# A hybrid encoder block on one core: branch A's query tiles taken two at a time in TensorE's hand-written order

## The chip, the cores and the metric

The kernel runs on one core of one Trainium2 chip. The metric is the time of one execution on the device in microseconds (us), the median of several runs. Lower is better. The engines are called as in the profile: PE (TensorE; PEld is its weight load), DVE (VectorE), ACT (ScalarE), POOL (GpSimd) and SP (SyncE, which issues the DMAs).

## The reference

One encoder layer is applied to a prompt of 2048 tokens and a sample of 512 tokens, with shared weights; 16 learned meta tokens stand ahead of each. Two attention branches are computed side by side, gated, projected and merged:

```python
u = rms_norm(h, norm_g)
proj = u @ w_in
qa, ka, va, za, qb, kb, vb, zb, ga, gb = jnp.split(proj, cuts, axis=-1)
o_a = neighbourhood_attention(qa, ka, va, na_rpb, n)      # 8 heads of 64, on a grid 64 wide
o_b = window_attention(qb, kb, vb, t5_bias, sink, n)      # 8 query heads, 2 key heads, +-128 tokens
y_a = (o_a * jax.nn.silu(za)) @ w_proj_a
y_b = (o_b * jax.nn.silu(zb)) @ w_proj_b
merged = jax.nn.sigmoid(ga) * y_a + jax.nn.sigmoid(gb) * y_b
h = h + merged @ w_out
return rms_norm(h[:, N_META:], final_g)
```

In branch A a grid token attends to a neighbourhood of 8 rows by 16 columns of the grid and to the meta tokens, with a learned bias. In branch B a token attends to 128 tokens on either side, the meta tokens and a sink. All is float32; each matmul operand is split into a high and a low float32r part, and products are summed from three matmuls (high by high, high by low, low by high).

## The kernel before, in words

The 2560 tokens are five windows of 512 (window 0 is the sample). A first phase, some 985 us long, computes the projections and writes queries, keys, values and gates to DRAM. The second phase does the attention, and between its pieces the dense work: the gates of the last window, the output projections of both branches, the last matmul and the final norm. After it comes a short end for the last window.

The attention's work is cut into units, one query tile of 128 each. `units` lists them window by window: first 32 units of branch A (four pairs of heads p, two heads h, four column groups g; `unit_a`, line 1047), then 16 units of branch B (two key heads gh, four tiles n, two head pairs i; `unit_b`, line 1143). A unit is a generator that gives back control after each of five steps:

- load: the DMAs of its keys, values and bias, where it is the first that needs them (g == 0);
- scores: two matmuls into a bank of PSUM (lines 1089, 1090; for branch B lines 1195, 1196, for two heads), the bias and the maximum on DVE (line 1020), the exponential with its sum on ACT (line 1027);
- normalise: the reciprocal on DVE (line 1031) and a multiplication into the tile `pr`, on DVE (line 1038), for g == 1 on ACT (line 1036);
- transposes: two to four blocks of `pr` through PE into a bank of PSUM called `tp` (line 1113; branch B line 1215, 1218), copied by ACT into the high part `ph` (line 1116) and by DVE into the low part `pl` (line 1117; branch B lines 1222, 1223, and 1232 to 1234 for the meta tokens, `pms`);
- products: values by probabilities into the one bank of `ps_o` (lines 1128, 1130; branch B lines 1239 to 1244). In branch A the four units of a head add up in the bank: the unit with g == 0 issues no product, and after g == 3 the bank is emptied by ACT (line 1134) and DVE (line 1136). In branch B each unit empties the bank: ACT copies one half (`ol`, line 1246), and DVE adds the halves with two additions (`y`, line 1249).

The first unit of B of each window gives control back once more, between the scores of its two heads (line 1191).

PSUM holds two banks for scores (`ps_s`), three for `tp` (`ps_p`; in branch A every third unit's scores use one of these), one for products (`ps_o`) and two for dense work (`ps_d`). A dense step is six matmuls of 128x512 (two calls of `mm3`, lines 144 to 146). A bank of a branch's output projection (`psa`, `psb`) takes two steps, one of the last matmul (`pso`) four. A finished `psb` bank is multiplied by the gate's tile `sgb`, which a DMA loads, on DVE (line 1304). The weights come through `Weights`: ACT writes the high part (line 198), POOL the low part (line 199). `phases` says which dense work belongs to which window and branch, `fill(amount)` runs as many dense steps as have come due. With a share of 0.5 for each half of a unit of A, one unit gets one dense step; in window 0, with 40 steps for 32 units, it is 0.625 each; in B one unit gets two steps. Five steps (`HELD`) are left over from B of window 0 for A of window 1, and so on.

The loop at line 1521 writes PE's order out by hand (`manual_schedule` for PE). The other engines' orders, SP's with its DMAs among them, are laid out by the framework from the order of the program and its own estimate of times. For the unit i, the loop asks for: the load of i + 4, the scores of i + 2, the normalising of i + 1, a fill, the transposes of i, a fill, and the products of i - 1. PE's order is so: scores of i + 2, transposes of i, a dense step, products of i - 1. Just before branch B one unit of B gets an extra step, because of its extra stop.

Of the kernel before, what the change touches and what calls it, by code (L numbers as in the profile page):

```python
# [95 lines left out]
def encoder_block(ctx: ExitStack, tc: tile.TileContext, xT, x_end, w_in, w_pa, w_pb, w_o, norm_g, final_g,  # L96
# [42 lines left out]
    def move(out, in_):  # L139
        last_move[0] = nc.sync.dma_start(*(f32(a) if a.dtype == F32R else a for a in (out, in_)))  # L140
        return last_move[0]
# [66 lines left out]
    class Weights:  # L208
# [16 lines left out]
        def next(self):  # L225
            i = self.i
            self.i += 1
            self.fetch(i + 2)
            self.split(i + 1)
            return self.wt.pop(i)  # L230
# [1211 lines left out]
    def phases(w, br):  # L1442

        if br == "a":
            if w == 0:
                yield from islice(gates, GATES_A)
            else:
                yield from dense_pb(w - 1)
                yield from dense_out(w - 1, range(0, 4))
        elif w == 0:  # L1450
            yield from gates
            open_dense()
            yield from dense_pa(0)
        else:
            yield from dense_out(w - 1, range(4, 8))
            pa = dense_pa(w)
            yield from islice(pa, 1)
            yield from with_fill(pa, dense_fin(w - 1))
# [7 lines left out]
    units = []  # L1466
# [31 lines left out]
    with tc.manual_schedule(engines={E.PE}):  # L1498
        N = len(units)
        dense, key, due = iter(()), None, 0.0  # L1500

        def fill(amount):
            nonlocal due
            due += amount
            while due >= 1 and next(dense, "end") != "end":
                due -= 1

        for i in range(1, 4):
            next(units[i][2])
        for _ in islice(gates, GATES_0 - 4):  # L1510
            pass
        for i in range(2):
            next(units[i][2])
        for _ in islice(gates, 4):
            pass
        vbm = vbm_d.rearrange("m g (h f) -> m g h f", h=2)
        for h in range(2):
            for r, part in ((0, 0), (32, 0), (64, 1)):
                move(vms[r + 16 * h : r + 16 * h + 16, :, h], vbm[:, :, part, :])
        next(units[0][2])  # L1520
        for i in range(N):
            br, w, _, weight = units[i]
            if key != (br, w):
                key, dense = (br, w), chain(dense, phases(w, br))
            if i == N - LAST:
                lo_eng[0] = nc.vector
            share = COUNT.get(key, 32) * weight / 32 / 2
            if i + 4 < N:
                next(units[i + 4][2])
            if i + 2 < N:  # L1530
                next(units[i + 2][2])
            if i + 1 < N:
                next(units[i + 1][2])
            fill(share)
            next(units[i][2])
            if [u[0] for u in units[i + 1 : i + 3]] == ["a", "b"]:
                next(units[i + 2][2])
            fill(share)
            if i:
                next(units[i - 1][2])  # L1540
        fill(2)
        next(units[N - 1][2])
        for _ in dense:
            pass
    attn.close()
# [105 lines left out]
```

## Time and profile before

| | us |
|---|---|
| median of 3 runs | 1888.8 (1888.74 to 1891.85) |
| time of the profiled execution | 1891.56 |
| its span from first to last instruction | 1889.7 |
| PE busy in the span | 1860.3 |
| DVE busy | 1316.7 |
| ACT busy | 1144.3 |
| POOL busy | 725.3 |

Branch A's transposes run from 992.8 to 1726.4 us of the span; A's five stretches are about 80 us long each, with B's between.

How to read it: all times are from one profiled execution, in us from the start of its span. A row of the timeline has the start, the duration, the engine, the line of the kernel, the operation, what it writes and what it reads, the shapes, a count (x4: four merged into one row), and in brackets how long the engine stood idle ahead of it and what ended that. The ends of matmuls are modelled, so that durations of neighbours overlap; the distance between two starts is what a matmul took of PE's time. A wait for several things is put down to the one that came last.

### The profile page before, as it was taken

The numbers are of one execution on the slowest core, as the hardware profiler recorded it, in microseconds if no ns is written. First come the engines' busy times: TensorE is split into PE (matmuls) and PEld (weight loads), VectorE is DVE, ScalarE is ACT, GpSimd is POOL, SyncE is SP. The second block draws the span as 40 slices with busy tenths as digits, with TensorE's granted clock in tenths as the row PEclk, the third lists the DMA queues.
The fourth block names the chain that finished last, engine by engine and source line by source line (L and its number), as shares of the span: only waits on it lengthen the run. The fifth ranks groups of instructions, "written<-read, shape, count | busy, mean of one in ns | idle before, by whom it ended". The sixth has DMA issues, their size and how long they took to land. (4 is left out here: it accounts for less than half of the span.)

```text
span 1889.7 us, 29760 instructions
## 1 busy us (share of the span) xinstructions
PE 1860.3 (98%) x9797; PEld 1585.9 (84%) x9797; DVE 1316.7 (70%) x2939; ACT 1144.3 (61%) x2523; POOL 725.3 (38%) x556
## 2 busy tenths in 40 slices
PE   8999999999999999999999999999999999999998
PEld 6898888888888887888878888888888888888886
DVE  8896666556477565444457888878787877888874
ACT  6454444434365443444456797797788778878932
POOL 2005442223202232232324435656744763685420
PEclk9999999999999999999999999999999999999999
DMA  7668666555296777744358878977985997697473
GB/s 262 227 173 306 195 181 191 192 194 179 81 333 228 234 214 203 205 140 156 110 193 311 275 213 263 298 220 247 314 281 177 313 314 226 218 315 257 119 296 138
DMA packets 290385, 424.83 MB, mean 225 GB/s; under 512 B 117416, under 2 KB 162040, under 8 KB 288696
## 3 DMA queue, kind: packets, MB, share of 16 engines
q1 hardware_dynamic: 289944, 422.93, 69.4%
q8 instruction: 78, 1.28, 0.3%
q14 instruction: 75, 0.61, 0.1%
q10 hardware_dynamic: 288, 0.01, 0.0%
HBM read 303.46 MB, written 119.39 MB: 224 GB/s over the span
## 5 line engine op out<-in xcount | busy, mean ns | idle before, releaser
L199 POOL TENSOR_TENSOR wt<-wraw,wt 128x512 fp32r<-128x512 f32 x164 | 213.3, 1319 | 266.5 <-ACT wt L198 264.9
L826 PE MATMUL pa<-u,wt 128*128 128x512 f32 x1008 | 242.7, 390 | 0.0
L826 PE MATMUL pa<-u,x 128*128 128x512 f32 x984 | 237.0, 390 | 1.7 <-ACT u L837 1.7
L198 ACT CAST wt<-wraw 128x512 fp32r<-128x512 f32 x312 | 177.9, 619 | 75.8 <-PE mm L146 37.4
L826 PEld LDWEIGHTS pa<-u,wt 128*128 128x128 f32 x1008 | 188.9, 188 | 39.1
L826 PEld LDWEIGHTS pa<-u,x 128*128 128x128 f32 x984 | 184.4, 188 | 41.1 <-ACT u L837 2.8
L797 POOL TENSOR_TENSOR s<-wraw,raw 128x512 f32<-128x512 f32 x40 | 58.3, 1458 | 274.5 <-DVE x L199 274.5
L144 PE MATMUL mm<-u,wt 128*128 128x512 f32 (+2 forms) x416 | 151.2, 363 | 7.8 <-ACT u L325 7.3
L792 POOL TENSOR_TENSOR s<-raw 128x512 f32<-128x512 f32 x40 | 58.4, 1459 | 255.4 <-DMA raw<-in_w_in_dram 252.1
L146 PE MATMUL mm<-u,wt 128*128 128x512 f32 (+2 forms) x416 | 147.6, 355 | 1.9 <-DVE wt L199 1.9
L145 PE MATMUL mm<-u,wt 128*128 128x512 f32 (+2 forms) x416 | 147.5, 355 | 1.1 <-DVE u L326 1.1
L199 DVE TENSOR_TENSOR wt<-wraw,wt 128x512 fp32r<-128x512 f32 x148 | 107.0, 760 | 49.5 <-ACT wt L198 49.4
L826 PE MATMUL pe<-u,wt 128*128 128x512 f32 x504 | 121.3, 389 | 0.0
L826 PE MATMUL pc<-u,wt 128*128 128x512 f32 x504 | 121.1, 389 | 0.0
L826 PE MATMUL pe<-u,x 128*128 128x512 f32 x480 | 115.3, 389 | 0.0
L826 PEld LDWEIGHTS pc<-u,wt 128*128 128x128 f32 x504 | 94.6, 188 | 19.6
L826 PEld LDWEIGHTS pe<-u,wt 128*128 128x128 f32 x504 | 94.5, 188 | 19.6
L1117 DVE TENSOR_TENSOR pl<-tp,ph 128x384 fp32r<-128x384 f32 (+6 forms) x160 | 94.8, 593 | 20.5 <-ACT ph L1116 18.0
L1116 ACT CAST ph<-tp 128x384 fp32r<-128x384 f32 (+6 forms) x160 | 81.7, 510 | 43.1 <-PE tp L1113 41.6
L144 PE MATMUL pso<-mh,wt 128*128 128x512 f32 x256 | 107.1, 418 | 0.0
L805 POOL TENSOR_TENSOR s<-wraw,s 128x512 f32<-128x512 f32 x40 | 54.9, 1373 | 132.7 <-DVE wt L199 132.7
L826 PEld LDWEIGHTS pe<-u,x 128*128 128x128 f32 x480 | 90.1, 188 | 18.7
(242 smaller groups left out, 4999.6 us busy)
## 6 DMA issues: line engine op xcount, KB each, us to landing
wraw<-in_w_in_dram SPq DMA_DIRECT2D x86, 512.0 KB
qa<-evq SPq DMA_DIRECT2D x20, 1024.0 KB
raw<-in_w_in_dram SPq DMA_DIRECT2D x40, 512.0 KB
q<-qa SPq DMA_DIRECT2D x20, 1024.0 KB
wraw<-in_w_o_dram SPq DMA_DIRECT2D x32, 512.0 KB
kbt<-kb SPq DMA_DIRECT2D x32, 384.0 KB
qb<-evq SPq DMA_DIRECT2D x20, 512.0 KB
ka<-evk SPq DMA_DIRECT2D x20, 512.0 KB
```

The costliest lines, as they stand in the source:

```text
L144: nc.tensor.matmul(ps, wh, uh, start=first, stop=False)
L145: nc.tensor.matmul(ps, wh, ul, start=False, stop=False)
L146: nc.tensor.matmul(ps, wl, uh, start=False, stop=last)
L198: nc.scalar.copy(h, r)
L199: low[0] = (eng or lo_eng[0]).tensor_sub(l, r, f32(h)).ins
L792: eng.tensor_add(s1, a21, a22)
L797: eng.tensor_sub(s3, a11, a21)
L805: eng.tensor_sub(s4, a12, s2)
L826: nc.tensor.matmul(ps, wt[:, a, s], u[:, b, kk, :], start=first and kk == 0 and i == 0, stop=kk == 3 and i == 2, skip_group_check=True)
L1116: nc.scalar.copy(ph_[:kb, a], tb)
L1117: nc.vector.tensor_sub(pl_[:kb, a], tb, f32(ph_[:kb, a]))
```

## The change

The loop takes branch A's units two at a time and leaves branch B's one at a time. For a pair (i, i + 1) of A it asks for: the loads of i + 4 and i + 5, the scores of i + 2, the normalising of i + 1, the products of the last unit of B if one is still open (`behind`), the transposes of i and of i + 1, the scores of i + 3, two dense steps' share, the normalising of i + 2, two more shares (so that a pair gets its two dense steps in one run, in window 0 two or three), and the products of i and i + 1. PE's order is so: scores of i + 2, transposes of i and i + 1, scores of i + 3, two dense steps, products of i and i + 1. At the last pair ahead of B (`change`) the two stops in the first B unit's scores are spread over the pair, and the second unit of B has its scores between the two dense steps. The number of steps of each unit and the dense work are the same.

```diff
         next(units[0][2])
-        for i in range(N):
+        def step(j):
+            if 0 <= j < N:
+                next(units[j][2])
+
+
+        i, behind = 0, -1
+        while i < N:
             br, w, _, weight = units[i]
             if key != (br, w):
                 key, dense = (br, w), chain(dense, phases(w, br))
             if i == N - LAST:
                 lo_eng[0] = nc.vector
             share = COUNT.get(key, 32) * weight / 32 / 2
-            if i + 4 < N:
-                next(units[i + 4][2])
-            if i + 2 < N:
-                next(units[i + 2][2])
-            if i + 1 < N:
-                next(units[i + 1][2])
-            fill(share)
-            next(units[i][2])
-            if [u[0] for u in units[i + 1 : i + 3]] == ["a", "b"]:
-                next(units[i + 2][2])
-            fill(share)
-            if i:
-                next(units[i - 1][2])
+            if br == "a":
+                change = units[i + 2][0] == "b"
+                step(i + 4)
+                step(i + 5)
+                step(i + 2)
+                step(i + 1)
+                step(behind)
+                step(i)
+                step(i + 1)
+                step(i + 2 if change else i + 3)
+                fill(2 * share)
+                if change:
+                    step(i + 3)
+                step(i + 2)
+                fill(2 * share)
+                step(i)
+                step(i + 1)
+                i, behind = i + 2, -1
+            else:
+                step(i + 4)
+                step(i + 2)
+                step(i + 1)
+                fill(share)
+                step(i)
+                fill(share)
+                step(behind)
+                i, behind = i + 1, i
         fill(2)
-        next(units[N - 1][2])
+        step(behind)
         for _ in dense:
             pass
```

## The prediction

> **What bounds the kernel now.** I read the page first: the span, and which engine fills it.
>
> ```profile
> span 1889.7 us, 29760 instructions
> PE 1860.3 (98%) x9797; PEld 1585.9 (84%) x9797; DVE 1316.7 (70%) x2939; ACT 1144.3 (61%) x2523; POOL 725.3 (38%) x556
> ```
>
> TensorE (PE) is the bound. The change touches only the stretches in which branch A runs, one for each of the five windows, so next I asked for the busy times in those five stretches (columns: length, then PE, PEld, DVE, ACT, POOL, the granted clock, DMA share, GB/s). Two of them and the sum of all five:
>
> ```profile
> core 0: us, PE busy (x) PEld busy (x) DVE busy (x) ACT busy (x) POOL busy (x), PEclk, DMA share, GB/s
> 1308.00:1394.00 86.00, 83.69 (x498) 72.11 (x498) 69.77 (x180) 66.13 (x151) 60.88 (x49) 1.00 1.03 316
> 1478.00:1563.00 85.00, 83.15 (x497) 71.68 (x496) 69.69 (x179) 65.56 (x147) 59.10 (x48) 1.00 1.03 315
> sum 414.00, PE 408.47 PEld 355.00 DVE 336.70 ACT 313.27 POOL 267.34; mean PE 81.69 PEld 71.00 DVE 67.34 ACT 62.65 POOL 53.47
> ```
>
> PE is idle for 414.00 - 408.47 = 5.5 us in all of branch A, 4.2 of it in the two quoted stretches (windows 2 and 3), where the DMA share is 1.03. The clock is 1.00, so there is none to win. The instructions of the transposes' line (L1113) say what most of the idle time is: four waits.
>
> ```profile
> L1113 PE MATMUL tp<-ident,pr x528: 270/272/302, 992.8 to 1726.4; 128*128 128x128 f32 x102, 128*96 128x128 f32 x37, 128*104 128x128 f32 x37
> DVE pr L1038: 4.2, 4
> ```
>
> So an order of PE's work can win in two ways: if neighbours in the order cost something where the operation changes, or by taking away those 4.2 us. Everything else it does can only add waits.
>
> **Neighbours.** Per pair of tiles, before: scores, transposes, dense step, products, twice. After: scores, both transposes, scores, two dense steps, both products. The matmuls are the same. The timeline of PE (start, duration; x4 is four merged) shows transposes followed by a dense step, and one place where transposes are followed by scores, as they will be:
>
> ```profile
> 1161.54 0.60 PE L1113 MATMUL tp<-ident,pr 128*96 128x128 f32 x4
> 1161.89 0.48 PE L144 MATMUL psb<-yb,wt 128*128 128x512 f32 x1
> 1162.21 0.40 PE L145 MATMUL psb<-yb,wt 128*128 128x512 f32 x1
> 1162.44 0.40 PE L146 MATMUL psb<-yb,wt 128*128 128x512 f32 x1
> ...
> 1221.58 0.29 PE L1196 MATMUL s<-kbt,q 128*128 128x274 f32 x1
> 1221.71 0.60 PE L1113 MATMUL tp<-ident,pr 128*96 128x128 f32 x4
> 1222.06 0.38 PE L1195 MATMUL s<-kbt,q 128*128 128x274 f32 x1
> 1222.28 0.30 PE L1196 MATMUL s<-kbt,q 128*128 128x274 f32 x1
> ```
>
> Durations have modelled ends; starts are what counts. Four transposes take 0.60 with the last lasting 0.272, so they start (0.60 - 0.272)/3 = 0.109 apart; dense matmuls start 0.23 apart (1162.21 to 1162.44). The first dense matmul looks expensive (0.48), but from the first transpose to the second dense matmul it is 1162.21 - 1161.54 = 0.67, and 4 x 0.109 + 0.23 = 0.67: the switch is free, the long first matmul is only the short last transpose (0.35 - 3 x 0.109 = 0.02) given back. At the second place, 1222.28 - 1221.71 = 0.57 = 4 x 0.109 + 0.13, the 0.13 being what such scores take (1221.58 to 1221.71): free as well. There are 160 tiles, so 80 meetings of transposes and dense work vanish; at the 0.004 us by which these sums are uncertain that is **-0.3 us**, bounds 0 and -1.6 (0.02 each, the one remainder seen).
>
> **From branch B to branch A (4 places).** The diff moves the products of the last tile of B, step(behind), ahead of A's first transposes, before any dense step. Products of B go to the one bank of ps_o, and each tile's products need that bank emptied of the tile before: a copy on ACT (L1246), then two additions on DVE (L1249). Before, one such place on three engines:
>
> ```profile
> 1477.53 0.28 PE L1244 MATMUL ob<-pl,vb 128*64 128x256 f32 x1
> 1477.65 0.40 PE L1089 MATMUL s<-kd,q 128*128 128x512 f32 x1
> 1478.13 0.49 PE L1113 MATMUL tp<-ident,pr 128*128 128x128 f32 x3
> 1479.85 0.28 PE L1239 MATMUL ob<-ph,vb 128*128 128x256 f32 x1
> ...
> 1477.85 0.37 ACT L1246 COPY ol<-ob 64x256 f32<-64x256 f32 x1 [0.30 <-PE ob L1244]
> ...
> 1478.25 0.58 DVE L1249 TENSOR_TENSOR y<-ob,ol 64x128 f32<-64x128 f32 x2 [0.71 <-ACT ol L1246]
> ```
>
> The bank is free at 1478.25 + 0.58 = 1478.83. Today transposes and a dense step lie between, and the next products start at 1479.85 without a wait. After, they stand at 1478.13, right behind the scores: a wait of 0.70. Behind it in PE's queue stand A's transposes, so nothing fills it. The same two marks (first transposes, then the additions) at the other three places:
>
> ```profile
> 1146.85 0.49 PE L1113 MATMUL tp<-ident,pr 128*96 128x128 f32 x3
> 1308.31 0.49 PE L1113 MATMUL tp<-ident,pr 128*128 128x128 f32 x3
> 1646.89 0.49 PE L1113 MATMUL tp<-ident,pr 128*104 128x128 f32 x3
> ...
> 1147.64 0.58 DVE L1249 TENSOR_TENSOR y<-ob,ol 64x128 f32<-64x128 f32 x2
> 1308.76 0.58 DVE L1249 TENSOR_TENSOR y<-ob,ol 64x128 f32<-64x128 f32 x2 [0.44 <-ACT ol L1246]
> 1647.72 0.58 DVE L1249 TENSOR_TENSOR y<-ob,ol 64x128 f32<-64x128 f32 x2
> ```
>
> They give 1.37, 1.03 and 1.41; with 0.70, **+4.5 us**. Bounds: 2.8 (all like the cheapest) and 5.6 (all like the dearest); a gain is excluded, because the chain of copy and additions can't begin before the products end.
>
> The Trainium skill (Perfetto Trace Analysis, section Matmuls) asks that independent groups of matmuls rotate through different PSUM banks, so that emptying one overlaps the next group's matmuls. By that rule each place would expose the whole emptying, 0.37 + 0.58 = 0.95 from the rows above, 3.8 us in four places in place of my 4.5; before, the trace shows no wait there although the bank is one, since other work lay between.
>
> **From A to B (5 places).** The second tile of B follows the first tile's second head with one dense step between; before, A's products lay there too. Both heads' banks must have been read by the exponentials on ACT:
>
> ```profile
> 1392.14 0.35 PE L1196 MATMUL s<-kbt,q 128*128 128x402 f32 x1
> 1394.04 0.28 PE L1128 MATMUL oa<-ph,v 128*128 128x256 f32 x1
> 1394.88 0.34 PE L1195 MATMUL s<-kbt,q 128*128 128x402 f32 x1
> ...
> 1394.30 0.21 ACT L1027 ACTIVATION_READ_ACCUMULATOR prs<-s,nm 128x1 f32 x1
> ```
>
> The second head's bank was free at 1394.51 and wanted at 1394.88: 0.37 to spare. From 1394.04 four products at 0.12 go elsewhere, so it is short by 0.1; and now the evictions of two A tiles stand ahead of those exponentials, a 0.5 copy on ACT and as much on DVE more. So 0.1 to 1.1 each; taken 0.5 each, **+2.5 us**, bounds 0 and 5.5. No gain, as nothing waits there today.
>
> **Inside the pairs.** The odd tile's products now follow its transposes after one pair of scores and two dense steps. The tightest place today (window 2):
>
> ```profile
> 1311.22 0.60 PE L1113 MATMUL tp<-ident,pr 128*128 128x128 f32 x4
> 1313.05 0.33 PE L1089 MATMUL s<-kd,q 128*128 128x384 f32 x1
> 1313.40 0.60 PE L1113 MATMUL tp<-ident,pr 128*128 128x128 f32 x4
> 1315.23 0.34 PE L1128 MATMUL oa<-ph,v 128*128 128x256 f32 x2
> ...
> 1314.07 0.69 DVE L1117 TENSOR_TENSOR pl<-tp,ph 128x512 fp32r<-128x512 f32 x1 [1.13 <-ACT ph L1116]
> ```
>
> Transposes to products: 4.01 today. After: 4 x 0.109 + 0.35 (1313.05 to 1313.40) + 12 x 0.23 = 3.55, so 0.46 less; the data is ready at 1314.76, 0.47 ahead. That spends all of it, and the even tile's eviction now comes just ahead of it (about 0.5 on ACT), so this place loses about 0.5. Windows 2 and 3 hold 16 such places and most will have more room; I take two like the tightest, **+1 us**, bounds 0 and 16 x 0.5 = 8. What hides the rest is the two dense steps, 2.76 us, while ACT and DVE empty both tiles.
>
> **The four waits for DVE.** One of them, on SP's queue, DVE and PE:
>
> ```profile
> 1343.41 0.34 SPq L140 DMA_DIRECT2D sgb<-gb  x1
> ...
> 1349.45 0.69 DVE L1304 TENSOR_TENSOR sgb<-psb,sgb 128x512 f32<-128x512 f32 x1 [2.35 <-DMA sgb<-gb]
> ...
> 1351.48 0.52 PE L1113 MATMUL tp<-ident,pr 128*128 128x128 f32 x3 [1.23 <-DVE pr L1038]
> ```
>
> The gate's tile takes 6 us to land while the DMA engines are full; DVE, which runs in order, stands for 2.35 us, and the normalised tile that PE wants is behind it. The change moves no bytes and the loads keep their distance of four tiles, so the DMA stays as late. But five dense steps are held over into A (HELD), an odd number, so a run of two ends one bank with its first step and opens the next with its second; that second step (6 x 0.23 = 1.38) and the products then lie between the instruction that DVE waits with and the next transposes: cover for about half. Taken **-2 us**; bounds -4.2 (all gone) and +4.2 (late at as many places again).
>
> Sum: -0.3 + 4.5 + 2.5 + 1 - 2 = +5.7 us. The profiled execution took 1891.56, 1.86 more than its span, and would take 1897.3; the median of the runs is 1888.8, 2.76 below it, and carries the same difference: **1894.5 us**, 0.3% slower.
>
> **The rivals.** First, on the other side: the late gate's tile decides. If the second dense step and the products cover all four of its waits, and B's last additions come at their cheapest in DVE's order, the sum is -1.6 + 2.8 - 4.2 = -3.0, so 1885.8: not slower, and with another 0.8 won it is faster. It decides from the point where the cover, 1.38 and the products' 0.5, is longer than the 1.23 that PE waited. For it speaks that 1.88 is more than 1.23, and that DVE and ACT are idle for a fifth of these stretches; against it, that DVE then has up to 2.35 us of work piled up behind the late instruction, and that the bank's ends need not fall on the first step of a run. Second, the pairs bunch the evictions: two copies, two subtractions and two maxima arrive at once, and in windows 2 and 3 all 16 odd tiles wait 0.5, which is 8 in place of 1, while none of the DMA's waits goes: 5.7 + 7 + 2 = +14.7, so 1903.5. For it speaks the spare time of 0.47; against it, that this was the tightest place of all. Third, the change does nothing that can be told: won and new waits cancel, 1885.0 to 1892.6. That the order is not what the diff says is no case: PE's order is written out by hand.
>
> **How the numbers follow.** What a measurement of this kernel can tell is about 0.2%, 3.8 us: below 1885.0 is faster, above 1892.6 slower. My forecast's case (1892.6 to 1899) has 0.40, bunching 0.12, cancelling 0.25, the first rival 0.23: its 1885.8 lies 0.8 above the limit, and as its terms are uncertain by more than that and PE's longer runs could add to it, I give 0.15 of it to faster and 0.08 to the same. So faster 0.15, same 0.33, slower 0.52. The range reaches from 1884.5 to 1901: it leaves out some of the first rival and the far end of the second. The forecast's own range is 1892 to 1899.
>
> **What would show it.** In the profile after: four waits of PE before L1239 for DVE y L1249, 0.7 to 1.4 us each, just ahead of A's first transposes; short waits of L1195 for ACT prs where A ends; spacing of transposes still 0.109 and the step into scores free; under L1113 fewer or shorter waits for pr. I am wrong if PE's dense matmuls start closer together than 0.23 in the longer runs, if the four waits for y are missing, or if L1113's waits grow beyond 4.2 us.

## The result, and the profile after

| | us | ratio to before, 95% interval |
|---|---|---|
| before, median of 6 runs beside the new kernel | 1890.36 (1888.74 to 1893.17) | 1 |
| after, median of 6 runs | 1899.70 (1896.91 to 1905.21) | 1.0049 [1.0034, 1.0064] |
| profiled execution before / after | 1891.56 / 1897.11 | |
| its span | 1889.7 / 1895.3 | |

The kernel is slower, by 9.3 us in the medians and by 5.6 us between the two profiled executions. The second figure is too small for what the change did: in the profile before, the attention began at 986.42 us of the span, in the profile after at 983.45, though nothing before it was changed. 1.6 us of these 3.0 come from a stretch of 3.4 us at half the granted clock near 60 us of the profile before (see the end): the same 22 dense matmuls take 6.73 us there (59.74 to 66.47) and 5.14 in the profile after. The new kernel's runs scatter by 8 us, and the slowest are those whose granted clock is lowest (1896.91 and 1897.11 at 0.999, 1904.16 and 1905.21 at 0.997; 0.002 x 1904 = 3.8 us, about half of the scatter). From the first scores of A to the last products of B the new kernel takes 8.25 us more. The page after, and then the busy times in just that stretch, before and after (columns as in the prediction):

```profile
span 1895.3 us, 29808 instructions
PE 1860.3 (98%) x9797; PEld 1586.6 (84%) x9797; DVE 1302.4 (69%) x2939; ACT 1141.3 (60%) x2523; POOL 724.8 (38%) x556
```

```profile
986.42:1808.94 822.52, 814.97 (x4938) 713.14 (x4938) 666.67 (x1889) 664.94 (x1671) 458.44 (x361) 1.00 0.81 254
```

```profile
983.45:1814.22 830.77, 816.32 (x4937) 714.78 (x4938) 652.58 (x1889) 661.53 (x1671) 457.84 (x361) 1.00 0.79 252
```

PE does the same work; its idle time went from 822.52 - 814.97 = 7.55 to 830.77 - 816.32 = 14.45 us. The other 1.35 us count as busy. The idle time in brackets begins at the modelled end of the matmul before: the scores ahead of the second wait below start at 1309.12 and end at 1309.52, though the next matmul could have started 0.23 behind them. And the first matmul behind a wait holds PE longer (from 1310.55 to 1310.74, 0.19 in place of the 0.12 of its kind). So a wait costs some 0.24 us more than its bracket says; nine new long waits against four lost ones make 1.2 of the 1.35, as an estimate. Look, then, for 6.9 us of new waits in brackets.

**B to A.** The four waits that the prediction named, on PE's timeline (in brackets the idle time and what ended it):

```profile
1147.38 0.36 PE L1239 MATMUL ob<-ph,vb 128*128 128x256 f32 x1 [1.35 <-DVE y L1249]
1310.55 0.36 PE L1239 MATMUL ob<-ph,vb 128*128 128x256 f32 x1 [1.03 <-DVE y L1249]
1480.38 0.36 PE L1239 MATMUL ob<-ph,vb 128*128 128x256 f32 x1 [0.69 <-DVE y L1249]
1650.03 0.36 PE L1239 MATMUL ob<-ph,vb 128*128 128x256 f32 x1 [1.38 <-DVE y L1249]
```

They sum to 4.45 us.

**A to B.** Here PE waits as well, but at another instruction than forecast: at the second set of transposes of A's last pair.

```profile
1068.54 0.41 PE L1113 MATMUL tp<-ident,pr 128*128 128x128 f32 x2 [1.80 <-DVE pr L1038]
1223.85 0.39 PE L1113 MATMUL tp<-ident,pr 128*96 128x128 f32 x2 [0.63 <-DVE pr L1038]
1391.34 0.52 PE L1113 MATMUL tp<-ident,pr 128*128 128x128 f32 x3 [0.86 <-DVE pr L1038]
1560.59 0.30 PE L1113 MATMUL tp<-ident,pr 128*128 128x128 f32 x1 [0.86 <-DVE pr L1038]
1728.28 0.29 PE L1113 MATMUL tp<-ident,pr 128*104 128x128 f32 x1 [0.79 <-DVE pr L1038]
```

4.94 us in all. DVE's timeline at the third of them says why:

```profile
1388.75 0.72 DVE L1038 TENSOR_SCALAR pr<-s,rd 128x512 f32<-128x512 f32 x1
1390.08 0.58 DVE L1020 CUSTOM_DVE_ANT_0 s<-s,bb 128x402 f32<-128x402 f32 x1 [0.60 <-PE s L1196]
...
1390.58 0.61 DVE L1038 TENSOR_SCALAR pr<-s,rd 128x384 f32<-128x384 f32 x1
```

DVE normalises the even tile, then stands idle for 0.60 us until PE has made B's first scores, takes their maximum, and only then normalises the odd tile, which PE wants next. DVE keeps the order it was given: the diff asks for the scores of unit i + 2 ahead of the normalising of i + 1. At the first of the five, in window 0, an instruction of the dense work (L282, 1.25 us at 1066.82) stands between the maximum and the normalising as well, which is why that wait is the longest, 1.80.

**The late gate's tile is gone.** What ended DVE's idle time at L1304 was, before, the DMA of `sgb` for 7.6 us in five places. After:

```profile
its engine sat idle before it (us, times) until:
  DMA sgb<-gb: 0.3, 1
```

The 4.2 us of waits for `pr` in windows 2 and 3, quoted in the prediction, went with it. 4.45 + 4.94 - 4.2 = 5.2 of the 6.9 us; the remaining 1.7 are the balance of short waits. Inside the pairs there are six, 1.4 us in all, the longest of them for `pl` at 1192.25 (0.33) and 1695.87 (0.36).

### The profile page after: what moved, and what is told of

The parts are those of the page before. It is cut to its first block, busy times and chain, and to the rows that moved or that the text cites. A ratio compares the mean times of both kernels' runs of the same rounds, so it can differ in the third digit from the quotient of the medians.

```text
span 1895.3 us, 29808 instructions
## 1 busy us (share of the span) xinstructions
PE 1860.3 (98%) x9797; PEld 1586.6 (84%) x9797; DVE 1302.4 (69%) x2939; ACT 1141.3 (60%) x2523; POOL 724.8 (38%) x556
## 4 chain that ended last, share of the span: by engine, by line
PE 79%; DVE 6%; DMA 4%; ACT 4%; issue 2%; POOL 2%; SPq 2%; ACTq 0%; DVEq 0%; POOLq 0%
PE pa L826 20%; PE pe L826 10%; PE pc L826 5%; PE mm L146 4%; PE mm L144 4%; PE mm L145 4%; PE tp L1113 3%; PE pso L146 2%; PE pso L144 2%; PE pso L145 2%; SPq L140 2%; DMA wos<-in_w_o_dram 2%; PE psb L145 2%; PE psb L144 2%; PE psb L146 2%
## 5 line engine op out<-in xcount | busy, mean ns | idle before, releaser
L1020 DVE CUSTOM_DVE_ANT_0 s<-s,ba 128x384 f32<-128x384 f32 (+5 forms) x160 | 86.9, 544 | 61.6 <-PE s L1090 60.5
L1027 ACT ACTIVATE prs<-s,nm 128x402 f32<-128x402 f32 (+1 forms) x160 | 91.1, 571 | 21.8 <-DVE nm L1020 18.8
```

Of the source, the lines that this page charges most:

```text
L1020: nc.vector.tensor_tensor_reduce(s[:, :n], s[:, :n], bias, -1.0, 3.0e38, ALU.add, ALU.min, nm)
L1027: nc.scalar.activation(out, s, AF.Exp, bias=nm, scale=-1.0, accum_out=sm)
```

## The experiments

Every ratio is to the kernel before on the same chip; one to four were run on one chip, five to eight on a second, nine and ten on a third. All edits but the fifth's are to the changed kernel.

### One: B's last products behind A's first transposes

```diff
-                step(behind)
                 step(i)
+                if behind >= 0:
+                    fill(2 * share)
+                    step(behind)
                 step(i + 1)
                 step(i + 2 if change else i + 3)
-                fill(2 * share)
+                if behind < 0:
+                    fill(2 * share)
```

At a window's first pair of A, the first tile's transposes and one dense step now lie ahead of B's products, the second tile's transposes behind them.

> The changed kernel, but at the first pair of A in windows 1 to 4 the last products of B come after A's first transposes and one dense step (as before the change), not right behind B's second-last products. Edge theory (the loss sits at the two borders between A and B): the four waits for DVE y, 4.5 us of gaps in the changed kernel, go; the ratio to before falls from 1.0049 to about 1.0023. Bunching theory (the loss is the pairs' bunched evictions, and a wait at a border only moves elsewhere): 1.004 to 1.005, with the lost time as other waits of branch A.

Measured: 1902.19 us, 1.0062 [1.0048, 1.0075]: not better than the change. The four waits for `y` are gone, but in windows 2 and 3 PE now waits for the normalised tile, and DVE ahead of it for the gate's tile again (L1304: DMA sgb 4.5 us, 4 times):

```profile
1350.92 0.30 PE L1113 MATMUL tp<-ident,pr 128*128 128x128 f32 x1 [0.63 <-DVE rd L1031]
1363.49 0.30 PE L1113 MATMUL tp<-ident,pr 128*128 128x128 f32 x1 [1.80 <-DVE pr L1038]
1533.74 0.30 PE L1113 MATMUL tp<-ident,pr 128*128 128x128 f32 x1 [1.43 <-DVE pr L1038]
```

3.9 us come back of the 4.45 won, and in the profile a drop of the granted clock costs 1.6 more (see the end). The expectation that the edge alone sets the price failed.

### Two: at A's last pair, normalise ahead of B's scores

```diff
-                step(i + 2)
-                step(i + 1)
+                step(i + 1 if change else i + 2)
+                step(i + 2 if change else i + 1)
```

> The changed kernel, but at the last pair of A in each window the normalising of the odd tile is asked for ahead of the scores of B's first tile, so that DVE takes pr before the maximum that waits for those scores. Edge theory: the five waits of the pair's second transposes for DVE pr, 4.9 us in the changed kernel, go; ratio about 1.0022. Bunching theory: DVE is simply behind with the two tiles, the waits stay at 3 us or more; ratio 1.004 to 1.005.

Measured: 1896.44 us, 1.0030 [1.0021, 1.0039]. The five waits for `pr` are gone, so DVE's order was their cause. 3.6 us are won by the ratios (0.0019 x 1890), not all 4.94: at one border the scores of B now wait for ACT, 0.32 us at 1068.65, the very wait that the prediction had expected there, and a late gate's tile costs 1.10 us at 1356.75. The profile is that of the fastest of the eleven runs (1892.76); the others may have waited more.

### Three: both edits together

> Both edits together; inside the windows the pairs stay. Edge theory: both terms go, 9.4 us of waits and some tenths around them, and what is left is the pairs' own balance, waits of about 3 us new against 4.8 us of waits for late DVE work lost: ratio 0.998 to 1.000. Bunching theory: 1.003 or more. A third case, that moving DVE's and SP's order brings back the late gate tiles: 1.001 to 1.002 with waits for pr of about 1 us in windows 2 and 3.

Measured: 1897.06 us, 1.0033 [1.0020, 1.0046], no better than the second alone. Both border waits are gone, and the late gate's tile is back in full; L1304 and PE's three waits behind it:

```profile
  DMA sgb<-gb: 7.8, 6
```

```profile
1347.27 0.30 PE L1113 MATMUL tp<-ident,pr 128*128 128x128 f32 x1 [1.37 <-DVE rd L1031]
1360.20 0.30 PE L1113 MATMUL tp<-ident,pr 128*128 128x128 f32 x1 [1.72 <-DVE pr L1038]
1530.29 0.30 PE L1113 MATMUL tp<-ident,pr 128*128 128x128 f32 x1 [1.97 <-DVE pr L1038]
```

### Four: another bank for B's last products, no order changed

```diff
-        o = ps_o.tile([P, WTOK], F32, tag="o", name="ob")
+        end = (gh, n, i) == (1, 3, 1) and w < NWIN - 1
+        o = (ps_p.tile([P, WTOK], F32, tag="tp", name="ob") if end else
+             ps_o.tile([P, WTOK], F32, tag="o", name="ob"))
```

> The changed kernel with its order, but the last unit of B of windows 0 to 3 writes its products to a bank of the transposes' pool in place of the one products bank. If the one bank is what makes PE wait at that border: the four waits for DVE y (4.5 us) go though nothing is moved, ratio about 1.0025, as for the moved products. If it is the time that the high and low parts of the transposes need: the waits stay, then for pl or pms, ratio 1.004 to 1.005. A transposes' bank may be missing for A's first transposes instead: up to 1 us at each of four places.

Measured: 1897.47 us, 1.0043 [1.0027, 1.0059]; the interval holds the change's own ratio. The four waits for `y` went without anything being moved, so the one bank was their cause. What is left of waits for `y` ahead of B's first products (L1239 in the changed kernel, L1241 here) is two places inside branch B's own stretches; first the changed kernel, then this run:

```profile
  DVE y L1249: 5.4, 6
```

```profile
  DVE y L1251: 0.9, 2
```

Most of what was won, 3.1 of 4.45 us, was given back in window 2, where the gate's tile is late again:

```profile
1347.65 0.30 PE L1113 MATMUL tp<-ident,pr 128*128 128x128 f32 x1 [1.05 <-DVE rd L1031]
1360.46 0.30 PE L1113 MATMUL tp<-ident,pr 128*128 128x128 f32 x1 [2.04 <-DVE pr L1038]
```

So whichever way this border's wait is removed, a gate's tile is late again in window 2. A likely reason is that PE now gets to it sooner than it lands; the next four experiments test that with a fourth buffer for the gate's tiles.

### Five: the kernel before, with four gate buffers

```diff
-        t = pools["d"].tile([P, WTOK], F32, tag="sg", name=name, bufs=3)
+        t = pools["d"].tile([P, WTOK], F32, tag="sg", name=name, bufs=4)
...
-                        sgs.append((pools["d"].tile([P, WTOK], F32, tag="sg", name="sgb", bufs=3) if f < 3 else
-                                    tl.tile([P, WTOK], F32, tag="sg", name="sgb", bufs=3)))
+                        sgs.append((pools["d"].tile([P, WTOK], F32, tag="sg", name="sgb", bufs=4) if f not in (4, 5) else
+                                    tl.tile([P, WTOK], F32, tag="sg", name="sgb", bufs=2)))
```

> The kernel before, its order untouched, with four buffers for the gate's tiles in place of three (and at the kernel's end another place for two of them), so that each gate tile is asked for one tile earlier. Theory (the four 1-us waits of the transposes in windows 2 and 3 come from a gate tile that lands late because its buffer comes free late): these waits go, DVE's group under L1304 shows no wait for DMA sgb, and 4.8 us are won: 1885.1 against 1889.9, ratio 0.9975. Rival (the DMA engines are full there, so asking earlier only makes another load late): the waits stay or move to q, kd or v, ratio 0.9990 to 1.0005.

Measured: 1889.58 us, 0.9999 [0.9988, 1.0009]. The rival holds in the main. DVE waits for no gate's tile any more, and the four waits of the transposes (4.2 us) are gone; but other loads are late. The first of these rows was there before too (0.77 us at 1007.45), the other two are new:

```profile
1006.93 0.37 PE L1089 MATMUL s<-kd,q 128*128 128x216 f32 x1 [1.01 <-DMA kd<-kam]
1365.77 0.42 PE L1089 MATMUL s<-kd,q 128*128 128x384 f32 x1 [1.32 <-DMA kd<-ka]
1555.63 0.42 PE L1195 MATMUL s<-kbt,q 128*128 128x402 f32 x1 [0.67 <-DMA xres<-in_xT_dram]
```

The scores in the last row do not read `xres`; the row names the transfer that ended last before they went. The stretch of attention is 821.21 us long in place of 822.52, so 1.3 us of the 4.8 were won there, too little to show in the medians.

### Six: the third experiment with four gate buffers

> The pairs with both borders repaired (the third experiment) and four buffers for the gate's tiles. Theory (what was left there, 5 us in windows 2 and 3, is the late gate tile, and apart from the borders a pair costs only some 3.5 us of short waits in its inside): the three long waits for DVE rd and pr at 1347, 1360 and 1530 go; 1890.36 - 4.8 + 3.5 = 1889, ratio 0.9993, and 1.002 times the kernel before with four buffers. Rival (the pairs' order itself makes DVE late, gate tile or not): the ratio stays at 1.003, with the waits for pr in place.

Measured: 1891.82 us, 1.0008 [1.0000, 1.0017]; with three buffers it was 1.0033. The three long waits are gone, and what ended PE's idle time ahead of the transposes is small:

```profile
  issue: 1.1, 6
  PE tp L1113: 0.7, 2
  PE s L1090: 0.3, 1
  DVE pr L1038: 0.2, 1
```

The rival, that the pairs' order itself makes DVE late, falls. The forecast of 0.9993 was 0.0015 too low.

### Seven: the changed kernel with four gate buffers

> The changed kernel as it is, with four buffers for the gate's tiles. Theory (its own order shows no late gate tile; its price is the borders, 4.45 and 4.94 us, and the inside): nothing is left to win, ratio 1.0045 to 1.005 as without the fourth buffer. Rival (the longer waits of PE at the borders and DVE's queue are themselves fed by late loads): they shrink, ratio 1.002 to 1.003.

Measured: 1897.77 us, 1.0043 [1.0030, 1.0055]. As expected, nothing to win that the interval could tell: the nine border waits are all there, within 0.02 us of those above.

### Eight: order and bank repaired, four gate buffers

The second and the fourth edit on the changed kernel, and four buffers.

> The pairs with the last tile of A normalised ahead of the first scores of B, the products of B's last tile in another bank (their place as in the changed kernel), and four buffers for the gate's tiles. Theory (three costs that add: bank, DVE's order, gate tile): all long waits go, and only the inside of the pairs is left: as the pairs with both borders moved, ratio 0.9993 (0.998 to 1.0005). Rival (some wait in windows 2 and 3 comes back whatever is removed, since the loads set the pace there): PE waits again for DVE rd or pr by 1 to 2 us at two to four places, ratio 1.002 to 1.004.

Measured: 1888.48 us, 0.9996 [0.9987, 1.0005]. Inside the forecast's bounds. The long waits at the borders and inside A are gone. One load is late, in window 2 just behind A:

```profile
1402.62 0.42 PE L1195 MATMUL s<-kbt,q 128*128 128x402 f32 x1 [1.58 <-DMA kbt<-kbm]
```

### Nine: order and bank repaired, three gate buffers

> The pairs with the norm ahead of the scores at the last pair and the other bank for the products of B's last tile, as in the eighth experiment, but with three buffers for the gate's tiles as in the changed kernel. Theory (with the borders repaired PE reaches the same gate tiles earlier than they land, and only a buffer more prevents it): DVE's multiplication of the gate waits for DMA sgb by 4 us or more in all, PE waits for DVE rd or pr in windows 2 and 3, ratio 1.002 to 1.004. Rival (the borders were the whole price, the fourth buffer is of no use, as it was of none in the kernel before): ratio 0.9992 to 1.0008, as with four buffers.

Measured: 1891.99 us, 1.0012 [1.0003, 1.0021], between the two forecasts. DVE waits for `sgb` for 2.5 us at two places, not 4, and PE once for long. DVE and PE at that place:

```profile
1344.96 0.69 DVE L1306 TENSOR_TENSOR sgb<-psb,sgb 128x512 f32<-128x512 f32 x1 [2.17 <-DMA sgb<-gb]
1345.57 0.74 DVE L1038 TENSOR_SCALAR pr<-s,rd 128x512 f32<-128x512 f32 x1
```

```profile
1346.46 1.24 PE L1113 MATMUL tp<-ident,pr 128*128 128x128 f32 x7 [1.82 <-DVE rd L1031]
```

The chain can be read off: the DMA lands, DVE multiplies the gate, normalises, and PE's transposes go. (The row of PE names `rd`, the last of DVE's results ahead of it; the tile `pr` of the row at 1345.57 was ready at 1346.31.) Without the fourth buffer most of the change's price is gone already. The difference to the eighth, 0.0016, is likely that of the late tile; the two intervals touch, so it is not shown.

### Ten: the eighth, with the loads of a pair's two tiles apart

```diff
                 step(i + 4)
-                step(i + 5)
...
                 fill(2 * share)
+                step(i + 5)
```

> The eighth experiment (both borders repaired, four buffers for the gate's tiles) with the loads of a pair's two tiles issued apart: those of the second tile half a pair later. Theory (loads that are asked for together make each other late; the eighth experiment has one late load left, kbt, for which PE stands 1.6 us): the wait for DMA kbt shrinks or goes and none takes its place: ratio to the kernel before 0.9982 to 0.9992. Rival (the DMA engines are full in windows 2 and 3 whatever the order, so what comes later lands later): PE waits for DMA kd, kbt or v by 1 us or more at one to three places, ratio 1.0000 to 1.0015.

Measured: 1888.80 us, 0.9999 [0.9991, 1.0008]: no gain. The wait for `kbt` stays (1.62 us at 1403.63), so asking for the loads together was not what makes it late.

No version beats both kernels by what can be told: the best of the pairs, the eighth, equals the kernel before.

## Why the prediction was right in its sign, step by step

- **Neighbours, -0.3: right.** In a run of twelve, dense matmuls start 0.228 apart (1317.87 to 1320.38 for eleven steps, in the profile after), as near to the 0.23 before as can be told; taking two tiles together has nothing to win at PE itself.
- **B to A, +4.5: right in place and cause, and nearly in size.** 4.45 us in brackets, with 0.7 to 1.4 at each place. That the two agree to 0.05 is in part luck: the prediction counted from start to start, and counted so the four places cost 5.1 (1.50, 1.20, 0.87 and 1.55), some 0.15 more each than the end of the additions had promised, still inside its bounds. The fourth experiment showed the cause by itself: with another bank the waits go, though nothing moves. That is what the rule on rotating banks asks for (the Trainium skill, Perfetto Trace Analysis, section Matmuls). By the rule alone the four places would cost 3.8; the measured 4.45 is nearer to the sum by places, which also counted how long copy and additions wait for their turn on ACT and DVE.
- **A to B, +2.5: the place was right, the waiting instruction and the size were not.** The step followed the exponentials on ACT and the banks of the scores. It did not follow DVE's order, in which the odd tile's normalising stands behind a maximum that waits for PE's own next scores. That cost 4.94 in brackets and, counted from starts, 5.7, above the bound of 5.5. The second experiment shows both: with the order turned, the five waits go, and the predicted wait for ACT appears, 0.32 us at one of the five places.
- **Inside the pairs, +1: about right.** 1.4 us in six short waits. With the borders repaired and no gate's tile late, pairs and single tiles cost nearly the same; the stretch of attention in the eighth experiment's profile, then in the fifth's:

```profile
984.20:1806.10 821.90, 815.00 (x4937) 715.19 (x4937) 651.48 (x1889) 660.32 (x1671) 458.36 (x361) 1.00 0.81 255
```

```profile
985.71:1806.92 821.21, 814.89 (x4937) 713.08 (x4938) 668.25 (x1889) 666.17 (x1671) 458.43 (x361) 1.00 0.80 255
```

Both hold waits for late loads (1.58 for `kbt` in the former, 1.01, 1.32 and 0.67 in the latter), so that the pairs' own balance is not known to better than some 2 us. But bunching, the second rival, is not what happens: it asked for 8 us of waits inside the pairs of windows 2 and 3, and the eighth experiment has none there; its four short ones (1.0 us) are in windows 0, 1 and 4.
- **The four waits for DVE, -2: the sign was right, the mechanism wrong.** "The DMA stays as late", it said, and the second dense step would cover half. DVE waited for a gate's tile once, for 0.3 us, and PE no longer behind it: -4.2, the end of its range. The step also paired the wrong rows. With three buffers used in turn, the multiplication at 1349.45 uses the tile that SP issued at 1339.97, not the one at 1343.41, so that it landed after 9.5 us and not 6. After, the tile for the multiplication at 1351.44 was issued at 1343.13, and 8.31 us were enough. SP's queue around the two, before and after:

```profile
1336.68 0.33 SPq L140 DMA_DIRECT2D wraw<-in_w_o_dram  x1
1339.04 0.33 SPq L140 DMA_DIRECT2D z<-za  x1
1339.97 0.33 SPq L140 DMA_DIRECT2D sgb<-gb  x1
```

```profile
1339.93 0.33 SPq L140 DMA_DIRECT2D wraw<-in_w_o_dram  x1
1342.69 0.35 SPq L140 DMA_DIRECT2D v<-va  x1
1343.13 0.74 SPq L140 DMA_DIRECT2D sgb<-gb  x1
```

The change moves the loads against each other and against PE. That the wait came back in the experiments that removed a border's wait, and went with a fourth buffer, shows that it hangs on when the tile is asked for and how soon PE gets there; the two were not told apart. Which transfer delays it in each case was not shown, and as each kernel has one profile, neither was how steady these late tiles are from run to run.

- **The sum.** +5.7 was forecast. In the profiles the attention takes 8.25 us longer: the border of A to B cost 2.4 more than forecast and the gate's tile won 2.2 more, which nearly cancel, by luck; the rest is 0.7 more in short waits (1.7 for the 1 inside the pairs), the 0.3 that neighbours did not win, and the 1.35 that count as busy, which the prediction left out. The medians say 9.3, so the measured 1899.70 lies just above the forecast's own range (1892 to 1899) and inside the wide one (to 1901). The 1.1 us between 8.25 and 9.3 are not explained. That the new waits bring drops of the clock in the other runs is likely from the last section, but not shown for them.
- **The signs that it named.** The four waits for `y` came. The short waits of L1195 for `prs` where A ends did not. And one of its signs of being wrong came, waits of L1113 beyond 4.2 us; after:

```profile
  DVE pr L1038: 5.6, 8
```

They are not the late tile's, which are gone, but the five of the border from A to B, 4.94 of the 5.6: the step that it had wrong.

- **The first rival** (the late tile decides, not slower) had the size right, all 4.2 us were won, but not by the cover that it named; but for 0.3 us once, the tiles had landed before DVE came to them. And the borders cost more.

## What to carry to other kernels

When two steps are put side by side on the engine that bounds, look at both ends of the new run: what lay between two uses of one bank there, and in which order another in-order engine gets its work, a maximum that waits for the bound engine itself above all. Where DMA is full, removing a wait can make PE reach the next load sooner, and a wait turns up there: in six experiments one did (one to five and nine). Follow a load from its issue to the instruction that uses it by counting through the buffers, not by the nearest row.

## What the runs showed of the hardware that was not expected

After a wait of PE of less than 2 us the granted clock can fall to half for 3.4 us. The ninth experiment's clock (the last column but two) in four stretches around the wait of 1.82 us:

```profile
1344.00:1346.50 2.50, 0.68 (x6) 0.39 (x5) 1.50 (x4) 0.03 (x1) 0.77 (x1) 1.00 1.02 240
1346.50:1348.00 1.50, 1.41 (x9) 1.11 (x10) 1.32 (x4) 0.88 (x2) 1.50 (x2) 1.00 1.00 269
1348.00:1351.40 3.40, 3.40 (x9) 2.65 (x8) 2.72 (x7) 1.95 (x6) 2.72 (x3) 0.50 1.03 370
1351.40:1353.00 1.60, 1.60 (x11) 1.40 (x10) 0.23 (x2) 0.69 (x1) 1.29 (x1) 1.00 1.02 413
```

In the third, dense matmuls start 0.43 apart in place of 0.23, so eight of them lose 1.6 us: the wait is paid nearly twice. The same happened in the first experiment behind a wait of 1.80 us (1071.5 to 1074.9), and in the seventh behind one of only 0.91 (1628.1 to 1631.5). It did not happen behind 1.80 us in the profile after, 1.97 in the third experiment or 2.04 in the fourth. So the length of the wait alone doesn't decide.

The records of the clock show most of what does. In all twelve profiles every drop begins a whole number of stretches of 3.413 us after the clock's first record (14 and 310 in the first experiment, 473 in the seventh, 14 and 391 in the ninth), so PE's idle time was added up within each such stretch. Ahead of the drops named here it was 1.80 us in the first experiment (1068.09 to 1071.51) and 1.91 in the ninth; near 60 us, where every profile has a wait of 1.4 to 1.9, it was 1.81 to 2.20 in the seven profiles with a drop and at most 1.72 in the five without. In the seventh it was 0.91, and behind that stand eight matmuls of a single column, which stretch over another 0.89 with hardly any work. The waits that brought no drop fall on two stretches: 1.72 of the 1.80 in the profile after lie in one, 1.60 of the 1.97, 1.43 of the 2.04. Two waits of 1.80 inside one stretch brought none either (at 1363.49 in the first experiment, at 1070.13 in the seventh), so the limit lies near 1.8 us here and is not known more exactly. The first record lies 10.9 to 13.7 us ahead of the first instruction, another time in each profile, so the same wait can bring a drop in one run and none in the next. No experiment moved a wait on purpose; this is read from the twelve profiles.

The Trainium skill (TensorE: Matmul & The Clock Gate, Part 1) has the clock fall after an idle window of about 3.4 us; the length of the drop agrees with that window, the idle time needed, about 1.8 us here, does not.
